# Moving four work tiles by 32 bytes in their partition: a prefix log-sum-exp kernel

## The chip, the cores and the metric

The kernel runs on one core of a Trainium2 chip. The metric is the device time of one execution in microseconds (us). The time before is the median of three runs; the profile is of one execution.

## What is computed

`x` has the shape (4, 4096, 4128) in float32. Along the second axis, the output is a running log-sum-exp, separately for each batch and column:

```python
out[:, 0, :] = x[:, 0, :].copy()
for t in range(1, S):
    mx = np.maximum(out[:, t - 1, :], x[:, t, :])
    out[:, t, :] = mx + np.log(np.exp(out[:, t - 1, :] - mx) + np.exp(x[:, t, :] - mx))
```

## The kernel before

The kernel exponentiates, forms prefix sums of the exponentials, and takes logarithms. It works in 49 steps. A step takes 256 or 384 consecutive rows of a batch: each of the 128 partitions holds two or three neighbouring rows (`r` = 2 or 3) of 4128 columns, so 33,024 or 49,536 bytes in one run, both in DRAM and in SBUF. The lists `begin`, `usual` and `final` say which step has how many rows.

A step's tile `xt` is worked on in place: it is loaded (L87), changed by ACT and DVE, and stored from the same tile (L90). There are four such work tiles in turn (`SLOTS = 4`): every fourth step uses the one tile of pool `x2` (two rows, 33,024 bytes a partition), the steps between use the three tiles of pool `x3` (room for three rows, 49,536 bytes a partition each). So 13 steps use the tile of `x2` and 12 each of the other three.

Within a step the columns are cut in three chunks of 1376. For each chunk ACT takes the exponential (L100), DVE adds the rows of a partition (L112 for three rows, L114) into a tile `z`, PE multiplies `z` with a triangular matrix of ones, which gives the sum over the partitions before and the carry of the step before (L122, into PSUM tile `pt`), DVE adds that to the rows (L131) and forms the last row's sum in `z` (L139, or L134 in a batch's last step), and ACT takes logarithms (L144, L145). In the first step of a batch ACT also writes a negated and clipped row into the tile `spare` (L103), only to get its sum in `short`; nothing reads `spare`.

The order on each engine is written out by hand in the lists `move`, `act`, `vec` and `pe`. SP issues all transfers on one queue: the loads of the first four steps, then store t and load t+3 in turn:

```python
moves = [("load", t) for t in range(SLOTS)]
ahead = SLOTS
for t in range(n):
    moves.append(("store", t))
    if t and ahead < n:
        moves.append(("load", ahead))
```

A load into a tile waits for the store that last used it, and a store waits for the logarithms of its step.

In a partition the tiles lie one behind the other in the order in which the pools were opened: the small constants with `spare` (L62), then the three `z` tiles, then the tile of `x2`, then the three of `x3`, without padding between the work tiles. In the built program the four work tiles start at bytes 39904 (`x2`), 72928, 172000 and 122464 (`x3`, in the order of their use).

Of the kernel before, what the change touches and what calls it, by code (L numbers as in the profile page):

```python
# [7 lines left out]
FP32 = mybir.dt.float32  # L8
# [13 lines left out]
def kernel(  # L22
# [8 lines left out]
    CH = D // NC  # L31
# [3 lines left out]
    consts = ctx.enter_context(tc.tile_pool(name="consts", bufs=1))  # L35
# [23 lines left out]
    nc.gpsimd.memset(probe, 1.0)  # L59

    short = consts.tile([1, B * NC], FP32, name="short")
    spare = consts.tile([1, CH], FP32, name="spare")  # L62
    tiny = consts.tile([1, 1], FP32, name="tiny")
    nc.gpsimd.memset(short, 0.0)
    nc.gpsimd.memset(tiny, SMALL)
# [251 lines left out]
```

## Time and profile before

| | before |
|---|---|
| median of 3 runs | 1263.09 us (1263.03 to 1263.58) |
| profiled execution | 1263.37 us, its span 1261.7 us |
| DMA queue of the loads and stores | 14112 packets, 541.07 MB, 99.5% of 16 engines' span |
| rate over the span | 429 GB/s, half read, half written |
| DVE, ACT, PE busy | 955.7, 955.4, 601.8 us |
| granted TensorE clock, mean | 0.680 |

The span runs from the first to the last instruction of the profiled execution. Busy times are those of the engines' instructions; the queue's share is the time that its packets took, divided by 16 times the span. A packet of this kernel is one partition's run of 33,024 or 49,536 bytes, or a completion mark of 4 bytes; the trace records the start and duration of each. The slices of the page each cover a fortieth of the span, so 31.5 us.

### The profile page before, as it was taken

To read this page: it belongs to the slowest core of one execution; us is meant where nothing else is said; L and a number is where in the kernel's file an instruction comes from. 1 tells how busy PE (TensorE), PEld (TensorE's weight loads), DVE (VectorE), ACT (ScalarE), POOL (GpSimd) and SP (SyncE) were. 2 spreads that over 40 slices of the span, in tenths; PEclk is the share of its full clock that TensorE was granted. 3 is DMA by queue.
4 is the path that set the end of the run, shared out by engine and by line. 5 is a ranking of instruction groups with operands and counts; after the bars stand their busy time and mean duration, and the time that the engine had idled before them with its cause. 6 is when DMAs were issued, how large, how long until landed. Compare 5 with 4: busy or idle time off the path is not lost.

```text
span 1261.7 us, 3428 instructions
## 1 busy us (share of the span) xinstructions
PE 601.8 (48%) x884; PEld 235.5 (19%) x884; DVE 955.7 (76%) x548; ACT 955.4 (76%) x466; POOL 4.6 (0%) x14
## 2 busy tenths in 40 slices
PE   3664454453645356345363545634534553463361
PEld 1221121121212122112121212211211211121120
DVE  3997696795966699579596679957957976795892
ACT  6987787786976698578697668867958966896792
POOL 1000000000000000000000000000000000000000
PEclk9876776667666666666676656666766676676776
DMA  9999999999999999999999999999999999999997
GB/s 402 419 438 426 434 431 433 429 430 435 433 429 435 428 437 438 427 436 434 428 435 428 441 429 430 439 432 431 436 432 431 431 435 430 436 433 431 431 436 333
DMA packets 14131, 541.28 MB, mean 429 GB/s; under 512 B 1568, under 2 KB 1568, under 8 KB 1568
## 3 DMA queue, kind: packets, MB, share of 16 engines
q1 hardware_dynamic: 14112, 541.07, 99.5%
q8 instruction: 7, 0.11, 0.0%
q14 instruction: 12, 0.10, 0.0%
HBM read 270.53 MB, written 270.53 MB: 429 GB/s over the span
## 4 chain that ended last, share of the span: by engine, by line
DMA 69%; ACT 14%; DVE 13%; PE 1%; issue 1%; SPq 0%; ACTq 0%; DVEq 0%
DMA xt<-in_x_dram 52%; DMA out_dram<-xt 17%; ACT xt L100 6%; DVE xt L131 5%; ACT xt L144 5%; DVE z L114 3%; ACT xt L145 3%; DVE z L139 3%; DVE xt L112 2%; PE pt L122 1%; SPq L90 0%; DVE z L134 0%; ACTq L144 0%; ACTq L100 0%; SPq L87 0%
## 5 line engine op out<-in xcount | busy, mean ns | idle before, releaser
L122 PE MATMUL pt<-z,carried 128*128 128x512 f32 (+1 forms) x810 | 551.4, 841 | 549.1 <-DVE z L114 549.1
L100 ACT ACTIVATE xt<-xt 128x4128 f32<-128x4128 f32 (+1 forms) x147 | 468.0, 3187 | 224.2 <-DMA xt<-in_x_dram 224.2
L122 PEld LDWEIGHTS pt<-z,carried 128*128 128x128 f32 x810 | 215.7, 283 | 884.7 <-issue 878.2
L131 DVE TENSOR_TENSOR xt<-pt,xt 128x2752 f32<-128x2752 f32 (+1 forms) x147 | 361.8, 2461 | 4.3 <-PE pt L122 4.3
L144 ACT ACTIVATE xt<-xt 128x2752 f32<-128x2752 f32 (+1 forms) x147 | 300.6, 2045 | 61.9 <-DVE z L139 57.1
L112 DVE TENSOR_TENSOR xt<-xt 128x1376 f32<-128x1376 f32 x90 | 142.8, 1587 | 221.2 <-ACT xt L100 221.2
L114 DVE TENSOR_TENSOR z<-xt 127x1376 f32<-127x1376 f32 x147 | 233.9, 1591 | 54.5 <-ACT xt L100 49.8
L139 DVE TENSOR_TENSOR z<-xt 128x1376 f32<-128x1376 f32 x135 | 214.9, 1592 | 4.6
L145 ACT ACTIVATE xt<-z 128x1376 f32<-128x1376 f32 x147 | 196.0, 1333 | 0.0
L122 PE MATMUL pt<-z,below 128*128 128x512 f32 (+1 forms) x72 | 50.2, 861 | 86.2 <-DVE z L114 86.2
L122 PEld LDWEIGHTS pt<-z,below 128*128 128x128 f32 x72 | 19.7, 291 | 116.1 <-issue 115.8
L134 DVE CUSTOM_DVE_ANT_0 z<-xt 128x1376 f32<-128x1376 f32 x12 | 19.1, 1592 | 0.4
L103 ACT ACTIVATE spare<-xt,tiny 1x1376 f32<-1x1376 f32 x12 | 17.3, 1441 | 0.5
L69 POOL MEMSET z<- 128x1376 f32 x3 | 3.7, 1242 | 0.0
L103 ACT ACTIVATION_READ_ACCUMULATOR spare<-xt,tiny 1x1 f32 x12 | 2.2, 185 | 0.0
L245 PE MATMUL good<-ones,low 128*1 128x1 f32 x2 | 0.2, 164 | 3.8 <-DVE low L243 3.8
L34 ACT ACT_TABLE_LOAD x1 | 1.3, 1283 | 0.8 <-PEq L301 0.8
L134 DVE DVE_READ_ACCUMULATOR2_ANT probe<- 128x1 f32 x12 | 1.0, 82 | 0.0
L245 PEld LDWEIGHTS good<-ones,low 128*1 128x1 f32 x2 | 0.1, 80 | 4.5 <-DVE low L243 4.5
L247 DVE TENSOR_SCALAR flag<-good 1x1 int32<-1x1 f32 x1 | 0.1, 147 | 0.3 <-PE good L245 0.3
L51 POOL TENSOR_SCALAR_AFFINE_SELECT carried<-below 128x128 f32<-128x128 f32 x1 | 0.3, 292 | 0.0
L45 POOL TENSOR_SCALAR_AFFINE_SELECT below<-below 128x128 f32<-128x128 f32 x1 | 0.3, 287 | 0.0
(13 smaller groups left out, 1.6 us busy)
## 6 DMA issues: line engine op xcount, KB each, us to landing
xt<-in_x_dram SPq DMA_DIRECT2D x30, 6192.0 KB, 38.8
out_dram<-xt SPq DMA_DIRECT2D x30, 6192.0 KB, 24.9
xt<-in_x_dram SPq DMA_DIRECT2D x19, 4128.0 KB, 33.1
out_dram<-xt SPq DMA_DIRECT2D x19, 4128.0 KB, 21.7
```

The lines of the kernel that those rows point to most:

```text
L34: nc.scalar.preload_act_table_set("natural_log_exp_and_others")
L69: nc.gpsimd.memset(t, 0.0)
L100: nc.scalar.activation(e, e, ACT.Exp)
L103: nc.scalar.activation(spare, t.xt[0:1, 0, self.cols], ACT.Relu, bias=tiny, scale=-1.0, accum_out=short[:, k:k + 1],)
L112: nc.vector.tensor_tensor(out=e[1], in0=e[0], in1=e[1], op=ALU.add)
L114: nc.vector.tensor_tensor(out=self.z[0:n], in0=e[r - 2][0:n], in1=e[r - 1][0:n], op=ALU.add,)
L122: nc.tensor.matmul(pt[:, a:b], lhsT=w, rhs=self.z[:, a:b], start=True, stop=True,)
L131: nc.vector.tensor_tensor(out=e, in0=base, in1=e, op=ALU.add)
L134: nc.vector.tensor_tensor_reduce(out=self.z, in0=ends[0], in1=ends[1], scale=1.0, scalar=0.0, op0=ALU.add, op1=ALU.add, accum_out=probe[:, ...
L139: nc.vector.tensor_tensor(out=self.z, in0=ends[0], in1=ends[1], op=ALU.add)
L144: nc.scalar.activation(e, e, ACT.Ln)
L145: nc.scalar.activation(t.xt[:, r - 1, self.cols], self.z, ACT.Ln)
```

## The change

The scratch tile `spare` is allocated 8 floats longer, and the kernel uses its first 1376 floats as before. Everything that is allocated behind it lies 32 bytes further on in the partition: `tiny`, the small tiles of the kernel's end, the three `z` tiles and the four work tiles, which now start at bytes 39936, 72960, 172032 and 122496. They lie 0, 0, 0 and 128 bytes past a multiple of 256 in the order of use, and 0, 0, 128 and 0 in the order in the partition; before, 224, 224, 96 and 224 in the order in the partition. Instructions and their order are the same on every engine.

```diff
     short = consts.tile([1, B * NC], FP32, name="short")
-    spare = consts.tile([1, CH], FP32, name="spare")
+    spare = consts.tile([1, CH + 8], FP32, name="spare")[:, :CH]
     tiny = consts.tile([1, 1], FP32, name="tiny")
```

## The prediction

> **What bounds the kernel now.** I read the page from the top: the busy shares, the slices, the DMA queues, then the chain and the DMA issues.
>
> ```profile
> span 1261.7 us, 3428 instructions
> ...
> PE 601.8 (48%) x884; PEld 235.5 (19%) x884; DVE 955.7 (76%) x548; ACT 955.4 (76%) x466; POOL 4.6 (0%) x14
> ...
> DMA  9999999999999999999999999999999999999997
> GB/s 402 419 438 426 434 431 433 429 430 435 433 429 435 428 437 438 427 436 434 428 435 428 441 429 430 439 432 431 436 432 431 431 435 430 436 433 431 431 436 333
> ...
> q1 hardware_dynamic: 14112, 541.07, 99.5%
> ...
> DMA 69%; ACT 14%; DVE 13%; PE 1%; issue 1%; SPq 0%; ACTq 0%; DVEq 0%
> ...
> xt<-in_x_dram SPq DMA_DIRECT2D x30, 6192.0 KB, 38.8
> out_dram<-xt SPq DMA_DIRECT2D x30, 6192.0 KB, 24.9
> xt<-in_x_dram SPq DMA_DIRECT2D x19, 4128.0 KB, 33.1
> out_dram<-xt SPq DMA_DIRECT2D x19, 4128.0 KB, 21.7
> ```
>
> The 16 DMA engines work 99.5% of the span, while the busiest compute engine works 76%. The chain names ACT and DVE for 27%, but that is a chain of causes: while they work, other transfers run. The table by stretches shows it. Its columns are the stretch and its length, busy time of PE, PEld, DVE, ACT and POOL, then clock, DMA share and GB/s.
>
> ```profile
> 0.00:63.00 63.00, 30.55 (x54) 12.54 (x54) 41.20 (x27) 50.95 (x33) 4.64 (x14) 0.89 0.98 411
> 378.00:504.00 126.00, 65.47 (x92) 24.98 (x93) 102.75 (x57) 100.40 (x47) 0.00 (x0) 0.63 1.01 435
> 1230.00:1262.00 32.00, 4.75 (x10) 1.73 (x8) 9.23 (x14) 8.62 (x7) 0.00 (x0) 0.60 0.76 328
> ```
>
> In the middle the DMA share is 1.00 and the compute engines rest a fifth of the time. Only the last stretch lets DMA engines stand idle. So the question is what one packet costs, and whether the start address of its tile enters that.
>
> The trace's record of the DMA packets answers the first half. One packet is one partition of one transfer: 4864 of 33,024 bytes (two rows) and 7680 of 49,536 bytes (three rows), so 304 and 480 for each of the 16 engines, with 98 completion packets. An engine's packets follow each other without a pause. From start to start it takes 1218.82 ns for the short and 1825.88 ns for the long. The difference, 607.06 ns for 16,512 bytes, is 27.20 bytes per ns; at that rate the short packet needs 1214.12 ns and the long 1821.18, so both leave the same fixed part of 4.70 ns. An engine's own work is 304 x 1218.82 + 480 x 1825.88 ns + 98 x 6 ns = 1247.5 us. The rest of the profiled time: the first packet starts at 1.8 us; the packets run over their usual length (1222 and 1829 ns as recorded, against means of 1227.9 and 1835.9) by 5.1 us an engine; an engine stands idle for 5.0 us on average, of which 4.1 us lie in the last 20 us; the last packet ends at 1259.4 and the span 2.3 us later. 1.8 + 1247.5 + 5.1 + 5.0 + 2.3 = 1261.7 us. Outside the span lie 1.67 us (1263.37 profiled), and the median of 1263.09 is 0.28 us below the profiled execution.
>
> **The change, part by part.** The built program has the same instructions in the same order on every engine. What moves is addresses: the four xt tiles go from 39904, 72928, 172000 and 122464 to 39936, 72960, 172032 and 122496, that is from 224, 224, 224 and 96 past a multiple of 256 to 0, 0, 0 and 128. The z tiles and the small ones behind `spare` move by the same 32 bytes. No wait is added.
>
> *Compute.* ACT, DVE and PE read and write at addresses 32 bytes higher, xt and z keeping their distances. No row shows what that does to a duration; the means by line (2461 ns at L131, 1592 at L139) hold tiles at 224 and at 96 alike. I take nothing. The cover: store 0 is issued at 37.64 us, while the four first loads hold an engine for 3 x 8 x 1218.82 + 8 x 1825.88 ns = 43.9 us, until 45.7, so 8 us are free. At the end the last store is issued here:
>
> ```profile
> 1242.85 0.33 SPq L90 DMA_DIRECT2D out_dram<-xt  x1
> ```
>
> The slowest engine ends its part of the store before it only at 1249.65, so compute may come 6.8 us later there before it costs anything; past that it costs one for one.
>
> *The fixed part of a packet.* It is 784 x 4.70 ns = 3.7 us an engine. The trace bounds it between untouched and gone: 0 to 3.7 us of gain. I take 0, by the nearest rows: the pitch of the long packets is 1825.86 to 1825.89 ns in each of the three large tiles, loads and stores, at 224 as at 96. If a start off the boundary cost something that grows with the distance, the tile at 96 would differ. What no row excludes is a cost that 224 and 96 share (both lie 96 past a multiple of 128); it stays in the range.
>
> A rule of the Trainium skill speaks here. The page "DMA: Bandwidth & Descriptors", section "How a descriptor splits into AXI transactions", says that a read must begin on a multiple of 256 bytes, and that bytes before the start are fetched and cost 32-byte beats. By it a store from 224 sheds seven beats and one from 96, now 128, gains one: at 607.06 ns / 516 = 1.18 ns a beat, (37 x 56 - 12 x 8) x 1.18 ns = 2.3 us an engine. The trace does not bear it out: seven beats are 8.2 ns, more than the whole fixed part of 4.70 ns, and loads of two rows, which read DRAM on multiples of 256, have the stores' pitch of 1218.8 ns.
>
> *Lateness of packets.* Of the 5.1 us, 3.6 us are 139 packets each more than 60 ns late, mostly in the first 30 transfers and in all tiles; I leave them. The other 1.6 us are small. Followed engine by engine (nine packets in ten can be placed), loads of three rows into the two tiles at 224 are 4.1 and 4.7 ns late on average, loads of two rows into the small tile 2.2, loads into the tile at 96 only 0.7. Stores: 1.0 to 1.7 ns everywhere. That looks like alignment, but much of it goes with the transfer ahead: in one and the same tile (the first of x3) loads are 5.8 ns late after a store of three rows and 1.8 after one of two, and loads into the tile at 96 always follow one of two. Like with like it is 1.8 against 0.7 ns, so 1.1 ns for 37 steps x 8 packets = 0.3 us. The whole difference between tiles would give 0.75 us; the stores of the tile at 96, 0.4 ns later than the others, speak for a loss of 0.2 us over 392 packets. I take 0.3 us of gain.
>
> Sum: 0 + 0 - 0.3: 1263.37 becomes 1263.1, and by the median 1262.8 us. What is late next after any gain: the 16 engines end the last store between 1253.5 and 1259.4 us, the early ones 9.75 us (eight packets) after its issue. If DMA engines became faster or even, the issue at 1242.85 would bound the end, so no gain from packets exceeds 5.9 us: 1257.2 us.
>
> **The rivals.** 0.2%, or 2.5 us, is about what a measurement of this kernel can tell from no change.
>
> *A start off a boundary costs every packet its fixed part.* For it: 224 and 96 are alike past multiples of 128 and of 64, and no tile of before lies on such a boundary. Against: loads from aligned DRAM and stores pay the same. Price 3.7 us and the 0.3: 1259.1 us. Chance 0.15.
>
> *Stores alone pay, by beats read before the start.* For it: nothing in a row but that short and long packets carry a fixed part at all. Against: the equal pitches above. At 2.3 us and the 0.3 it gives 1260.5, just past 0.2%. Chance 0.07. This is the skill's rule named above.
>
> *Packets get later (slower).* Place: loads that share the engines with stores of three rows. With all starts on one boundary, the packets of 16 engines could meet in DRAM in step, and the lateness of the worst group (6.5 ns, step 41's loads) spread to every packet. For it: lateness already hangs on the neighbour, and grows inside a load from its first packets to its last. Against: only 32 bytes move, and all DRAM addresses stay. 784 x (6.5 - 2.0) ns = 3.5 us more: 1266.6 us; it decides from 2.5 us / 784 = 3.2 ns a packet on, and a loss has no roof in the rows. Chance 0.17.
>
> That the change does not do what it says is ruled out by the addresses of the built program.
>
> **How the numbers follow.** The forecast, 1262.8 us, holds 0.61, its own range 1261.3 to 1264.4 (0.75 us of lateness and some unevenness of engines to either side). Faster is 0.15 + 0.07 = 0.22, slower 0.17. The range for 8 in 10 goes down to 1258.5, past the first rival, and up to 1266.6, the price of the slower one, which leaves out about half of the slower cases and the last of the faster ones.
>
> **What would show it.** Right: pitches of 1218.8 and 1825.9 ns, a queue share of 99.5%, the last issue near 1242.9 and the last packets near 1253.5 to 1259.4. The first rival: pitches shorter by some ns, in loads and stores. The second: in stores alone. The slower one: old pitches, more packets late, GB/s below 430 in the middle slices. The forecast is wrong if mean duration moves by over 3.2 ns a packet.

## The result and the profile after

The changed kernel takes 1261.51 us (median of 22 runs, 1260.98 to 1262.26) against 1263.05 us for the kernel before in the same comparison (22 runs, 1262.56 to 1263.82): a ratio of 0.9987, with a 95% interval from 0.9981 to 0.9993. That is 1.5 us or 0.13% faster: within the 0.2% that the prediction calls no change, though the interval ends below 1. The profiled execution took 1261.62 us.

The page after, in the lines that answer to those of before:

```profile
span 1259.9 us, 3428 instructions
...
PE 600.7 (48%) x884; PEld 234.8 (19%) x884; DVE 956.2 (76%) x548; ACT 955.5 (76%) x466; POOL 4.6 (0%) x14
...
DMA  9999999999999999999999999999999999999997
GB/s 403 419 440 424 431 435 429 428 437 434 434 431 441 424 437 439 428 436 435 427 443 425 440 424 437 440 434 435 425 439 432 427 434 428 440 433 430 430 439 339
...
q1 hardware_dynamic: 14112, 541.07, 99.5%
...
DMA 69%; DVE 14%; ACT 14%; PE 1%; issue 1%; SPq 0%; ACTq 0%; DVEq 0%
...
xt<-in_x_dram SPq DMA_DIRECT2D x30, 6192.0 KB, 38.6
out_dram<-xt SPq DMA_DIRECT2D x30, 6192.0 KB, 25.0
xt<-in_x_dram SPq DMA_DIRECT2D x19, 4128.0 KB, 33.2
out_dram<-xt SPq DMA_DIRECT2D x19, 4128.0 KB, 21.4
```

Nothing on the compute side has moved: DVE 956.2 us against 955.7, ACT 955.5 against 955.4. The queue still fills 99.5% of a span that is 1.8 us shorter. By stretches and at the end:

```profile
0.00:63.00 63.00, 29.90 (x54) 12.17 (x54) 41.01 (x27) 50.75 (x33) 4.64 (x14) 0.92 0.98 411
378.00:504.00 126.00, 67.09 (x94) 26.11 (x95) 103.39 (x57) 99.64 (x47) 0.00 (x0) 0.69 1.01 435
1230.00:1262.00 32.00, 4.23 (x8) 1.48 (x7) 6.53 (x11) 5.79 (x5) 0.00 (x0) 0.56 0.73 317
```

```profile
1240.02 0.33 SPq L90 DMA_DIRECT2D out_dram<-xt  x1
```

The last store is issued 2.8 us earlier (1242.85 before). The chain that the profile follows back from it runs through compute alone to the landing of the third load from the end, step 46's, after which ACT starts at 1179.02 us instead of 1181.81. The last load itself lands about 8 us before ACT takes it up, in both. The gain is in the record of single packets, which these views only sum up. Worked out from the trace as in the prediction ("usual" means no more than 1 ns over 1222 or 1829 ns; "small" sums the lateness of packets up to 60 ns late, "long" that of the others, both divided by 16 engines):

| | before | after |
|---|---|---|
| start to start, short and long packet | 1218.82, 1825.88 ns | 1218.82, 1825.88 ns |
| packets at usual length, short and long | 75%, 70% | 97%, 94% |
| small lateness an engine | 1.56 us | 0.39 us |
| long lateness an engine | 3.58 us | 3.48 us |
| mean idle time of an engine up to the last packet's end | 5.0 us | 4.4 us |
| last packet's end, earliest to latest engine | 1253.5 to 1259.4 us | 1251.8 to 1257.6 us |

The pace of back-to-back packets did not change by 0.01 ns. What went is small lateness: 1.2 us. Another 0.6 us is less idle time of the engines, in the last 20 us (4.1 us there before, 3.5 after). The first 63 us, where about half of the long lateness lies, move 411 GB/s as before.

### The profile page after: what moved, and what is told of

Same layout as the page of the kernel before. It is cut to its first block, busy times and chain, and to the rows that moved or that the text cites. A ratio compares the mean times of both kernels' runs of the same rounds, so it can differ in the third digit from the quotient of the medians.

```text
span 1259.9 us, 3428 instructions
## 1 busy us (share of the span) xinstructions
PE 600.7 (48%) x884; PEld 234.8 (19%) x884; DVE 956.2 (76%) x548; ACT 955.5 (76%) x466; POOL 4.6 (0%) x14
## 3 DMA queue, kind: packets, MB, share of 16 engines
q1 hardware_dynamic: 14112, 541.07, 99.5%
## 4 chain that ended last, share of the span: by engine, by line
DMA 69%; DVE 14%; ACT 14%; PE 1%; issue 1%; SPq 0%; ACTq 0%; DVEq 0%
DMA xt<-in_x_dram 49%; DMA out_dram<-xt 19%; ACT xt L100 6%; DVE xt L131 6%; ACT xt L144 5%; DVE z L114 3%; DVE z L139 3%; ACT xt L145 3%; DVE xt L112 2%; PE pt L122 1%; SPq L90 0%; DVE z L134 0%; ACTq L144 0%; ACTq L252 0%; ACTq L100 0%
```

## Experiments: which start addresses cost, and where

After the change both transfers of a step and all engines use moved tiles, so four things are open: which property of the address counts, which tile, which direction, and whether compute engines have a part in it. Theory *blocks* formed only after the first four runs; the first theories were *64* and *128* (a start off a multiple of 64 or 128 bytes is late) and *distance* (lateness grows with the bytes to the boundary below).

**All tiles 32 or 64 bytes past (e1_all32, e2_all64).** Only the length of `spare` differs:

```diff
-    spare = consts.tile([1, CH], FP32, name="spare")
+    spare = consts.tile([1, CH + 16], FP32, name="spare")[:, :CH]   # e1_all32
+    spare = consts.tile([1, CH + 24], FP32, name="spare")[:, :CH]   # e2_all64
```

> Work tiles at 32, 32, 32 and 160 past a multiple of 256 (64 bytes further than before). Theory 64: packets are late when a tile starts 32 bytes off a multiple of 64, whatever the rest of the address; then 72 of 100 packets keep their usual length, small lateness is 1.6 us an engine, and the time is that of before, 1263.0 us. Theory distance: lateness grows with the bytes to the 256 boundary below (224 before, 32 here); then small lateness falls to about a seventh of 1.2 us above the 0.4 us of the change, so 0.6 us, and the time to 1261.7 us.

> Work tiles at 64, 64, 64 and 192 past a multiple of 256. Theory 64: as the change, over 94 of 100 packets at their usual length, 0.4 us of small lateness, 1261.5 us. Theory 128 (a start off a multiple of 128 is what costs): as before, about 72 of 100, 1.6 us, 1263.0 us.

Measured: 1262.80 us (11 runs; small lateness 1.19 us) and 1262.67 us (11 runs; 0.95 us), both with a ratio to before of 0.9996 (0.9987 to 1.0005). None of the theories fits. With starts on multiples of 64 bytes much of the lateness remained, so theory 64 falls; theory 128 wanted 1.6 us for both, theory distance 0.6 us for 32. The two lie between, and sorting loads by tile shows why. Percentages are packets at usual length among those that can be placed:

```
loads of two rows into x2     start   0: 97%    32: 45%    64: 53%   224: 62%
loads of three rows into x3   start   0: 92-95%  32: 82-84%  64: 87-92%  96: 92%  128: 95%
                              start 160: 68%   192: 77%   224: 38-46%
```

About one packet in ten could not be placed, and those are late more often. All of them can be placed by the order of transfers, which is the same on every engine; then loads of three rows at 224 come to 27 and 37%, loads of two rows at 64 to 46% and at 224 to 57%, and the other shares of this and the following tables move by at most 5 points.

Three rows are mostly on time up to a start of 128 and late more often beyond, though the gap between 32 and 192 is small; two rows are on time from 0 alone. Three rows are 49,536 bytes, 193.5 blocks of 256: from a start up to 128 they touch 194 blocks, beyond it 195. Two rows are exactly 129 blocks, and any start but 0 makes it 130. So theory *blocks*: a packet that touches one more block of 256 bytes than it must is late.

**Only the work tiles (e3_xt_only).** `z` and the small tiles stay, the four work tiles move as in the change:

```diff
-    z = [zpool.tile([P, CH], FP32, name=f"z{c}") for c in range(NC)]
+    z = [zpool.tile([P, CH + 8 * (c == 2)], FP32, name=f"z{c}")[:, :CH] for c in range(NC)]
```

> Only the four work tiles move by 32 bytes; z and the small tiles stay where they were before. Theory 64 or 128 on the transfers: as the change, 0.4 us of small lateness and 1261.5 us. Theory compute (the addresses of z decide, through the engines): as before, 1.6 us and 1263.0 us.

Measured: 1261.49 us, ratio 0.9987 (0.9978 to 0.9996), small lateness 0.38 us. The work tiles do it alone, and theory compute falls.

**Only the tiles of x3, two ways (e4_x3_only, f3_x3_only).** The first made `xt` a flat tile, cut to rows afterwards; the second puts a gap between the pools and leaves the tile as it was:

```diff
-            full = self.pool.tile([P, rows, D], FP32, name="xt")
-            self.xt = full[:, :self.r, :]
+            full = self.pool.tile([P, rows * D + 8 * (rows == 2)], FP32, name="xt")      # e4_x3_only
+            self.xt = full[:, :self.r * D].rearrange("p (j d) -> p j d", j=self.r)
...
+    ctx.enter_context(tc.tile_pool(name="gap", bufs=1)).tile([P, 8], FP32, name="gap")   # f3_x3_only
     x3 = ctx.enter_context(tc.tile_pool(name="x3", bufs=3))
```

> Only the three tiles of x3 move by 32 bytes; the tile of x2 stays at 224. Theory own address: only packets of steps in the tile of x2 are late (about 2.2 ns in loads, 1.0 ns in stores), those of the others not; small lateness 0.4 us plus 13 steps x 8 x 3 ns = 0.3 us, 0.7 us in all, and 1261.8 us. Theory neighbour: late packets are spread by the transfer in front, so loads into the x3 tile that follow a store from x2 (the third x3 tile) become late and loads after a store of three rows do not.

> Once more only the three tiles of x3 moved by 32 bytes (to 0, 0 and 128) with the tile of x2 at 224, now with a gap between the pools, so that tiles keep their shape and every wait is that of before. If the 15 us of the first try came from its waits, they are gone: 1261.9 us. Theory blocks: only loads of two rows into x2 are late (about 60 of 100 at their usual length), those of three rows are not (over 90); small lateness 0.7 us. Theory mixed starts (tiles of unlike alignment disturb each other): again over 1270 us with long lateness over 60 ns.

Measured: 1277.99 us for the first (4 runs; ratio 1.0118, 1.0103 to 1.0134), 1262.37 us for the second (11 runs; 0.9994, 0.9985 to 1.0003). The work tiles start at the same addresses in both, and every engine runs the same operations in the same order. The flat tile changed which instructions wait for which: in the first program engines wait where they did not before. Two rows of the waits of e4_x3_only, with the time in all, how often, and the longest:

```profile
ACT xt L144 <- DVE z L139: 151.9, 81, 7.8
...
DVE z L139 <- ACT xt L100: 25.5, 8, 3.2
```

Before, the second was not among the waits at all, and the first stood at:

```profile
ACT xt L144 <- DVE z L139: 57.1, 66, 6.0
```

Early on this leaves the queue empty. The stretch from 40 to 65 us, by the columns explained in the prediction, in e4_x3_only and then in f3_x3_only:

```profile
40.00:65.00 25.00, 17.55 (x32) 6.96 (x31) 23.91 (x16) 25.00 (x17) 0.00 (x0) 0.80 0.81 349
```

```profile
40.00:65.00 25.00, 13.35 (x27) 5.01 (x26) 22.91 (x15) 25.00 (x15) 0.00 (x0) 0.84 0.99 411
```

A DMA share of 0.81 for 25 us is 4.7 us lost there; in all the engines stand idle 13.0 us instead of 5.0. Long lateness rose as well, from 3.58 to 8.8 us; it goes with the other waits, since f3_x3_only has the same addresses and 3.9 us, but how was not tried. So the first try says nothing on addresses, and theory mixed starts falls. The second fits theory blocks in the main: loads into x2 at usual length 70%, of three rows 85 to 93% where over 90 was expected, small lateness 0.74 us as expected, and a time 0.5 us above the expected one, with 3.9 us of long lateness.

**Where the step lies for three rows (f1_x3_96, f2_x3_160, g3_all0).** The tile of x2 at 0, the three of x3 all at 96, at 160 or at 0:

```diff
...                            # pad(bytes, name) allocates a tile that nothing uses
+    pad(32, "gap")
     x2 = ctx.enter_context(tc.tile_pool(name="x2", bufs=1))
-    x3 = ctx.enter_context(tc.tile_pool(name="x3", bufs=3))
+    pad(96, "gap0")            # f2_x3_160: 160, g3_all0: 0
+    x3 = []
+    for c in range(3):
+        x3.append(ctx.enter_context(tc.tile_pool(name=f"x3{c}", bufs=1)))
+        pad(128, f"gap{c + 1}")
...
-            pool = x3 if len(steps) % SLOTS else x2
+            pool = (x2, *x3)[len(steps) % SLOTS]
```

> The tile of x2 at 0 past a multiple of 256, all three tiles of x3 at 96; waits and order as before. Theory blocks: a load is late only when its packet touches one block of 256 bytes of SBUF more than it must. 49,536 bytes are 193.5 blocks: from a start up to 128 they touch 194, from a later one 195. 33,024 bytes are 129 blocks: from 0 they touch 129, from any other start 130. So here loads of three rows and loads into x2 keep their usual length in over 90 of 100 packets, only the six steps of two rows in tiles of x3 are late; small lateness 0.5 us, time 1261.6 us. Theory start (any start off a multiple of 128 is late): loads of three rows in all three tiles are late, small lateness 1.2 us or more, 1262.7 us.

> As the kernel with the tiles of x3 at 96, but all three at 160. Theory blocks: loads of three rows touch 195 blocks and are late in all three tiles (under 70 of 100 at their usual length), those into x2 are not; small lateness 1.2 us or more and 1262.7 us, a full 1 us slower than with 96. Theory start: as with 96, since both lie 32 bytes off a multiple of 64; no difference between the two kernels.

> The whole kernel with all four work tiles at 0 (128 bytes of padding between the tiles of x3). Theory blocks: three-row packets touch 194 blocks from 0 as from 128 and from 96, so nothing is gained on the change: small lateness 0.4 us, 1261.5 us. Theory start (only a multiple of 256 is free): the tile that the change leaves at 128 gains, some 0.2 to 0.3 us.

| | x3 at 96 | x3 at 160 | x3 at 0 | the change (0, 0, 128) |
|---|---|---|---|---|
| three-row loads at usual length | 94-95% | 31-66% | 93-95% | 92-95% |
| small lateness an engine | 0.37 us | 1.42 us | 0.38 us | 0.39 us |
| median | 1261.47 us | 1262.68 us | 1261.81 us | 1261.51 us |
| ratio to before (95% interval) | 0.9988 (0.9979-0.9997) | 0.9999 (0.9990-1.0008) | 0.9988 (0.9979-0.9997) | 0.9987 (0.9981-0.9993) |

96 is as good as 0 and 160 as bad as before, from tiles 64 bytes apart. That is what theory blocks forecast for three rows. Against it stands one thing: loads of two rows into a tile of x3 at 96, which touch a block too many, are 88% on time (66% at 160), where theory blocks had them late; so the extra block alone does not fix how late a load is. A rival was not tried: that it is the size of the pieces in the first and last block that counts. Three rows leave pieces of 128 bytes or more at starts of 0 to 128, and smaller ones, 32 to 96 bytes, at 160 to 224; two rows leave a piece of 32 to 96 bytes at every start tried but 0. So both theories sort all these starts alike, and neither tells two rows at 96 from two rows at 160. Nothing is gained by putting all four tiles at 0, and no version beats the change by more than its spread.

**Which direction, and without compute (f4_load224, f5_store224, g1_both0, g2_both224).** The 98 transfers alone: loads alternate between two tiles, stores read a third that holds ones. The four kernels differ only in where these lie.

```diff
...
+    def load(t):
+        xt = (la, lb)[t % 2].tile([P, 3, D], FP32, name="xt")
+        nc.sync.dma_start(out=xt[:, :steps[t][2], :], in_=dram(x, steps[t]))
+    def store(t):
+        nc.sync.dma_start(out=dram(out, steps[t]), in_=source[:, :steps[t][2], :])
...
+    load(0)
+    load(1)
+    for t in range(n):
+        store(t)
+        if t + 2 < n:
+            load(t + 2)
...
```

> Transfers alone: the 49 loads and 49 stores of the kernel without its arithmetic. Loads go into two tiles at 224, stores come from a third tile at 0 that holds ones, so the output is not the reference's. Theory blocks on the writing side: loads are late as before, without any compute engine at work (under 70 of 100 at their usual length), and stores mostly not. Theory reading side (stores pay for a start off a block): loads and stores are both on time, over 94 of 100. Theory engines (ACT and DVE on the same tile delay the transfers): all on time here.

> The same transfers alone, loads into two tiles at 0, stores from a tile at 224. Theory blocks on the writing side: all on time, over 94 of 100 packets at their usual length. Theory reading side: the stores are late, under 70 of 100, and their start-to-start time may grow by the beats that are read for nothing (8.2 ns).

> Transfers alone, no arithmetic, loads into two tiles at 0 and stores of ones from a tile at 0 (the output is not the reference's). Theory blocks on the writing side: small lateness 0.2 us an engine as with stores from 224. Open is the long lateness (over 60 ns late), which was 2.9 us with loads at 224 and stores at 0 and 4.9 us with loads at 0 and stores at 224, in one look each. If the start of the stores' tile makes it, it is about 2.9 us here and the time some 1258 us; if the start of the loads' tile makes it, 4.9 us and some 1263 us; if it is chance, its times spread by several us.

> Transfers alone, loads into two tiles at 224 and stores of ones from a tile at 224. Theory blocks on the writing side: small lateness 1.9 us, as with stores from 0. Long lateness: 4.9 us if the start of the stores' tile makes it, 2.9 us if that of the loads' tiles makes it, spread over several us if chance.

The page of f4_load224 shows that no compute engine has a part: DVE fills the stores' tile at the start, and the queue is as full as ever.

```profile
DVE 10.5 (1%) x3; POOL 0.2 (0%) x4
...
q1 hardware_dynamic: 14112, 541.07, 99.7%
```

| loads / stores at | 224 / 0 | 0 / 224 | 0 / 0 | 224 / 224 |
|---|---|---|---|---|
| three-row, two-row loads at usual length | 36%, 47% | 97%, 96% | 98%, 99% | 44%, 54% |
| three-row, two-row stores at usual length | 81%, 95% | 97%, 99% | 98%, 98% | 79%, 91% |
| small lateness an engine | 1.89 us | 0.18 us | 0.14 us | 1.76 us |
| long lateness an engine | 2.86 us | 4.94 us | 2.74 us | 3.47 us |
| time | 1260.22 us (1 run) | 1263.88 us (1 run) | 1258.48 us (5 runs) | 1261.55 us (10 runs) |

The start of the tile that a load writes makes the small lateness, with all compute engines at rest. The start of the tile that a store reads makes none: with loads at 0, stores from 224 keep their usual length in 97% and more, and their start-to-start time is 1218.82 and 1825.88 ns in all four kernels. Where loads are late, stores next to them are a little late too. With both at 0 the transfers take 3.1 us less than with both at 224: 1.6 us of small lateness, 0.7 us of long, 0.8 us of engines waiting for the slowest.

The long lateness is not settled. The stores' start alone does not make it (4.94 us against 3.47 us, both with stores at 224), nor the loads' alone (4.94 against 2.74 us, both with loads at 0), and each is one profile. The columns 224 / 0 and 0 / 224 were also taken on one chip and the other two on another, so a difference of chips is not ruled out; small lateness, 1.89 and 1.76 us with loads at 224, was alike on both. In 0 / 224 long lateness lay on six engines with 8 to 10 us each while the lowest seven had 1.2 to 2.0 us, and the slowest engine ended 9.7 us after the first. Whether that one time of 1263.88 us is chance was not tried.

## Why the prediction was right, and where it was off

It gave 1262.8 us with a chance of 0.61 for no change by 0.2%; 1261.51 us lies within that 0.2% and inside the forecast's own range, 1261.3 to 1264.4, near its lower end. The sign was right and the size a fifth of what came: 0.3 us forecast, 1.5 us measured. That the time stayed within 0.2% did not hang on this size: all the small lateness of before is 1.56 us, worth about 2 us at the rate given below, less than the 2.5 us of 0.2%.

*Compute: nothing.* Right: the durations by line and the busy times stayed, and the transfers without any arithmetic show the same effect.

*The fixed part of a packet: nothing.* Right to 0.01 ns. With it fall the first rival, whose 3.7 us hung on it, and the second. The rule of the Trainium skill (page "DMA: Bandwidth & Descriptors", section "How a descriptor splits into AXI transactions") gave the second its 2.3 us for reads that start off a multiple of 256 bytes; no run here shows such a cost in reads, and stores from 224 run at the pace of stores from 0. Blocks of 256 bytes do matter here, but on the side that writes SBUF, and not as a fixed price for each packet.

*Lateness of packets: 0.3 us.* This is the term that was mis-sized: small lateness fell by 1.17 us. The prediction saw the difference between the tiles at 224 and at 96, worth 0.75 us by its count, and then gave most of it to the store ahead of a load. With every packet placed, the loads were 1.08 us late an engine before, nearly none of it in the tile at 96, and 0.10 us after: the whole difference between the tiles went. The neighbour does matter in the trace of before, but as something that makes an unfavourable start worse: after the change, loads of three rows into the first tile of x3 that follow a store of three rows are 84 to 96% on time, where it had been 9 to 38%. The tile at 96, by its block count already a good one, showed what the others could become. The prediction compared it only with loads that follow a store of two rows (1.8 against 0.7 ns), took that 1.1 ns for all 37 steps, and so left out what loads after a store of three rows had to lose (5.8 ns). Stores, in which the prediction saw a hint of a loss of 0.2 us and took nothing, gained 0.2 us in all (0.48 to 0.29 us); the transfers alone show that stores are late beside late loads and not by their own start.

*Unevenness of engines.* The prediction let the slowest engine set the end, and took no change. The engines' idle time fell by 0.6 us, which with 1.17 us of small and 0.1 us of long lateness gives about the 1.8 us of the span. Only the small lateness is shown to hang on the starts: f1_x3_96 and g3_all0, alike in it, differ by 0.5 us in idle time, with one profile each. Over the nine versions of the whole kernel that keep its waits, time falls by about 1.2 us for each us of small lateness (1.56 us at 1263.05, 1.42 at 1262.68, 1.19 at 1262.80, 0.95 at 1262.67, 0.74 at 1262.37, 0.37 to 0.39 at 1261.47 to 1261.81; all within 0.3 us of a straight line).

*The end.* Two readings of it were wrong. The prediction took the issue of the last store, 1242.85 us, as a bound that stays where it is, so that no gain from packets could go below 1257.2 us. The issue came at 1240.02 us, because it hangs on the landing of earlier loads and moves with them. And the early engines end the last store 10.7 us after its issue, not 9.75: its first packet starts 0.8 us after the issue. So of the signs that it named, the pitches and the queue's share held, while the last issue and the last packets (1251.8 to 1257.6 us) came 1.7 to 2.8 us earlier than before.

*The slower rival.* Lateness was indeed the quantity that moved, but it fell where that rival let it spread. With all four tiles on one boundary (g3_all0), small lateness is 0.38 us.

Open: whether it is the extra block or the small pieces at its ends that delay a packet, and by what mechanism, why the delay grows inside a load and with the store ahead, and what makes the long lateness.

## What to carry to other kernels

Where a queue is full for the whole span, look at single packets: the most frequent duration tells the pace, the share of packets that keep it tells what disturbs them. Where such a queue bounds the time, try placing a tile that is loaded so that its run per partition touches as few blocks of 256 bytes as its length allows; here that was worth 0.13%, cost 32 bytes, and mattered for loads, not for stores. When an experiment reshapes a tile to move it, look at the waits before reading its time: here 15 us came with them.

## What the runs showed of the hardware that was not expected

Loads that wrote one block of 256 bytes too many kept their usual duration in 31 to 77% of packets (three rows, starts of 160 and more) instead of 92 to 95% where every tile started well, yet the commonest duration and the start-to-start time were the same in every kernel, 1218.82 and 1825.88 ns. Stores showed nothing of the kind by their own start: from 224, with loads at 0, 97% and more kept it. And lateness over 60 ns, which no start explained, was spread very unevenly over the 16 engines in the profile of loads at 0 and stores at 224: 1.2 to 10.4 us each.
